# First mixer of a one-core fp32 layer stack: values of four heads opened in 512-wide matmuls, a new order of the later values and of one gate tile, and recurrence steps emitted within a tick

## The chip, the core and the metric

The kernel runs on one core of a Trainium2 chip. The metric is the device time of one execution in microseconds (us); several executions give a median. Five engines matter: TensorE (PE, with its weight loads shown as PEld), VectorE (DVE), ScalarE (ACT), GpSimd (POOL) and SyncE (SP), which issues the loads. TensorE's clock has two levels, 1.2 and 2.4 GHz, and the profile gives the granted share of the upper one (PEclk). Each engine runs its own instructions in the order in which the program emitted them, and waits for the others through semaphores.

## What is computed

The reference is a layer stack on x of 1024 tokens by 1024 features: a gated linear recurrence (the first mixer), an MLP, a dilated attention (the second mixer), a second MLP. The change lies in the first mixer alone, which is, cut to what matters:

```
proj = h @ w_in;  q, f, i, g = split(proj, 4)          # 8 heads of 128
k  = (1 - lb) * sigmoid(-f);  log_f = log(lb + (1 - lb) * sigmoid(f))
qf = silu(q) * 128 ** -0.5
S_t = diag(f_t) S_{t-1} + k_t v_t^T;   o_t = S_t^T q_t    # v = i, per head
o  = o * rsqrt(mean(o^2) + eps) * out_norm * silu(g)
return o @ w_out
```

## The kernel before, in words

All products are fp32 made of three fp32r matmuls (`mm3`, L212 to L214: high by high, high by low and low by high parts). The tile is 128 rows of contraction by 128 by 512 or 256 columns. Weights come as slabs of 128 by 1024 through `use` and `split_next`: a load (SP), a cast of the high part (ACT, L175) and a subtraction for the low part (DVE, L178).

The recurrence of a head is made parallel: within 32 tokens directly (`diag`), then by levels that join blocks (`level0`, `level1`, `level2`, then `level(16)`, `level(32)`, `level(64)`), and over chunks of 128 tokens by states (`krt` transposes the keys, `states`, `outs`), with a norm and a turn (`scale`, `final`) at the end. Each level issues a small group of matmuls that scores queries `qf` against keys `kr` (L367 and L413 and L485), and then on DVE brings both forward: `advance` (L401 to L403) and `queries` (L386 to L390) for the queries, `keys` (L442, L443), `totals` (L432 to L434) for the decays, `keep` (L420) which copies scores under a mask, and L492 to L494 for the three upper levels. So each level reads on PE what DVE wrote in the level before.

These steps are emitted between the large matmuls. `unit` (24 matmuls of 512 columns) and `unit_b` (48 of 256 columns in two halves) call `tick` in their middle or at the end of each half; `tick` runs what stands in the plan for that slot, in the order in which it was put there. The table `SCAN_AT` gives each of the twelve steps of a head its tick, counted from the end of the head's queries. A head takes 8 ticks (four units: f in two halves, q in two halves), and the steps of a head stretch over 24, so steps of two or three heads interleave. Two heads share one pair of value tiles: before heads 0, 2, 4 and 6 the values of the pair are computed 256 columns wide with tokens on rows (192 matmuls), then f and q of both heads. I call these stretches pair 1 (heads 0 and 1) to pair 4; the values that follow a pair (or the gate tiles after pair 4) run while its second head's steps are due. For f, DVE scales the bank (L609), ACT makes `f`, `kr` and `f` again (L783 to L785). For q, DVE scales (L609), ACT takes a sigmoid (L794), and DVE multiplies (L795) into `qf`.

The program opens with the values of heads 0 and 1 for the first 512 tokens, one slice of contraction at a time as x and the weights arrive.

Of the kernel before, what the change touches and what calls it, by code (L numbers as in the profile page):

```python
# [11 lines left out]
F32 = mybir.dt.float32  # L12
F32R = mybir.dt.float32r
# [7 lines left out]
P = 128  # L21
# [76 lines left out]
class Kernel:  # L98
    def __init__(self, tc, ctx, x, w, consts, masks, tab, out):
        self.tc, self.nc = tc, tc.nc  # L100
        self.low = self.nc.vector
        self.x_dram, self.w_dram, self.c_dram = x, w, consts
        self.m_dram, self.tab_dram, self.out_dram = masks, tab, out
        cp = ctx.enter_context(tc.tile_pool(name="consts", bufs=1))
        self.cp = cp
        self.sm = ctx.enter_context(tc.tile_pool(name="small", bufs=2))
        self.tp = ctx.enter_context(tc.tile_pool(name="tmp", bufs=N_TMP))
        self.slots = Slots(ctx.enter_context(tc.tile_pool(name="slots", bufs=1)), N_SLOTS)
        self.acc = ctx.enter_context(tc.tile_pool(name="acc", bufs=4, space=bass.MemoryType.PSUM))
# [36 lines left out]

    def tick(self):
        while self.slot in self.plan:
            for fn in self.plan.pop(self.slot):
                fn()  # L150
        self.slot += 1

    def drain(self):
        while self.plan:
            self.tick()
# [198 lines left out]
    def hgrn_scan(self, h, qf, kr, f, v):  # L354
# [15 lines left out]
        def diag():  # L370
            ps = small(self.bank(), lambda t: qf[:, t:t + 32], 32)
            ve.copy_predicated(ac, self.masks[:, M_DIAG:M_N], ps)
            st["tots"] = S.get("tots")

# [17 lines left out]
        def advance(i, half, tot):  # L392
            b = B4[i]
            n = HALF // (4 * b)
            r = st.pop((i, half))
            rv = r[:, :768].rearrange("p (v n b) -> p v n b", v=6, b=b)
# [6 lines left out]
            ve.tensor_tensor(qv[:, 2:4], rv[:, 3::2], d0, op=MUL)  # L403
            S.put(r)

# [63 lines left out]
        def level(b):  # L469
# [4 lines left out]
            if b == 16:  # L474
                pv = small(ps, lambda t: qv[:, t // (2 * b):(t + 32) // (2 * b), 1, :], 16)
                ve.copy_predicated(ac.rearrange("p (n two b) -> p n two b", two=2, b=b)[:, :, 1, :],
                                   self.masks[:, M_16:M_DIAG].rearrange("p (n b) -> p n b", b=b),
                                   pv.rearrange("p (n b) -> p n b", b=b))
            else:
# [43 lines left out]

        t = SCAN_AT
        for i, fn in enumerate((diag, level0, level1, level2)):
            self.at(t[i], fn)
        for i in range(3):
            self.at(t[4 + i], lambda i=i: level(16 << i))
        for i, fn in enumerate((krt, states, outs, scale, final)):
            self.at(t[7 + i], fn)  # L530

# [110 lines left out]
    def run(self):  # L642
# [3 lines left out]
        x = [S.get("x") for _ in range(KT)]  # L646
        wst = [S.get("w") for _ in range(2)]
        self.next_load = 2

# [3 lines left out]

        def load_w(i, c0=0, n=HALF):
            c = slice((i % 2) * HALF + c0, (i % 2) * HALF + c0 + n)
            nc.sync.dma_start(wst[i // 2][:, c], self.w_dram[i // 2][:, c])

# [3 lines left out]
        load_w(0, 256, 256)  # L661
        load_x(1, 0)
        load_w(1)
        load_x(2, 0)
        load_x(3, 0)
        load_w(2)
        load_x(4, 0)
        load_x(5, 0)
        load_w(3)
        load_x(6, 0)  # L670
        load_x(7, 0)
        for k in range(KT):
# [25 lines left out]
        zs = [None, None]  # L698
        vs = [S.get("v"), S.get("v")]
        ws = [(S.get("hi", F32R), S.get("lo", F32R)) for _ in range(2)]  # L700
        banks = [self.accb() for _ in range(4)]

        def split_w(k, n):
            hi, lo = ws[k // 4]
            c = slice((k % 4) * 256, (k % 4) * 256 + n)
            nc.scalar.copy(hi[:, c], wst[k // 4][:, c])
            nc.vector.tensor_tensor(lo[:, c], wst[k // 4][:, c], hi[:, c].bitcast(F32), op=SUB)

        for k in range(KT):
            if k == 0:  # L710
                split_w(0, 256)
            self.split_x(x[k], self.col(C_NMIX + k), u[k], 0)
            if k and (k == 1 or k % 2 == 0):
                split_w(k, 256 if k == 1 else 512)
# [7 lines left out]
        S.put(*wst)  # L722
        self.next_split = self.next_use = 2
        self.at(0, self.split_next)
        for k in range(KT):
# [3 lines left out]
        bp = [self.bank() for _ in range(2)]  # L729
        self.unit_b(ws, u, 2, bp[0])  # L730
        self.col_b(ws, u, 6, range(KT), bp[1][:, :256])
        zs[0] = self.norm_rows(sqs, 0, self.rb, delay=0)
        for k in range(KT):
            self.square_in(x[k], k, 1, sqs, engine=nc.vector)
        for t in range(4):
            self.values1(banks[t], t, vs, zs[0])
        self.col_b(ws, u, 7, range(KT), bp[1][:, 256:])
        self.tick()
        self.blocks = sm.tile([P, P], F32R, name="blocks")
        self.ones = sm.tile([P, P], F32R, name="ones")  # L740
# [20 lines left out]
        def second_half():  # L761
            zs[1] = self.norm_rows(sqs, 1, self.rb, delay=1)
            for p in range(2):
                self.values(bp[p], 2 + p, vs, zs)
            S.put(*x, sqs)

        self.at(2, second_half)
        self.done(ws)
        for h in range(8):
            if h % 2 == 0 and h:  # L770
                vs = [S.get("v"), S.get("v")]
                ws = self.use(2)
                for p in range(4):
                    ps = self.unit_b(ws, u, p)
                    self.values(ps, p, vs, zs)
                self.done(ws)
            f, kr, qf = S.get("f"), S.get("kr"), S.get("qf")
# [11 lines left out]
            for half in range(2):  # L789
# [11 lines left out]
        for j in range(8):  # L801
# [7 lines left out]
            self.done(ws)  # L809
        self.drain()  # L810
        S.put(*self.a_bufs, self.rb)
# [957 lines left out]
```

## Time and profile before

| | us |
|---|---|
| median of 3 runs (lowest to highest) | 2263.52 (2262.01 to 2264.18) |
| the profiled execution, its own time | 2263.14 |
| its span in the profile | 2261.4 |
| PE busy | 2233.7 (99%) |
| DVE busy | 1775.9 (79%) |
| ACT busy | 856.0 (38%) |

The first mixer fills about the first 450 us of the span. PE is the engine that is nearly always busy, so time is read from PE: what its large matmuls take from one start to the next, and every stretch in which it stands. A PE row with idle time before it names in brackets what released it. The ends of matmuls are modelled and overlap, so the path is read from start to start.

### The profile page before, as it was taken

Reading aid. Unit: us, or ns where it says so; the run is one execution under the profiler, and the core shown is the slowest. Engines: PE = TensorE matmul, PEld = TensorE weight load, DVE = VectorE, ACT = ScalarE, POOL = GpSimd, SP = SyncE. Lnnn points to the kernel's source line nnn. Section 1 sums busy time; section 2 is a strip of 40 time slices with the busy share of each in tenths; the row PEclk is TensorE's granted clock in tenths of the full one; section 3 lists DMA queues with packets and bytes.
Section 4 is the critical chain, followed back from the end, with each engine's and each line's share of the span. In section 5 each row is a group of like instructions: output and inputs, shape, how many; then the busy total and the mean of one; then the engine's idle time right before and its main releaser. Section 6 shows DMA issues by size and latency. Waiting matters only on the chain.

```text
span 2261.4 us, 32861 instructions
## 1 busy us (share of the span) xinstructions
PE 2233.7 (99%) x13102; PEld 1883.5 (83%) x13102; DVE 1775.9 (79%) x2674; ACT 856.0 (38%) x1259; POOL 347.0 (15%) x340
## 2 busy tenths in 40 slices
PE   8999999999999999999999999999999999999998
PEld 7888897888888888888889888888888888888887
DVE  6757668736988888989996556885798888889896
ACT  6333333434433335433344232224533333634322
POOL 0020101101111111222210011000111111222223
PEclk9999999999999999999999999999999999999999
DMA  5001011122344448544514101113334445744442
GB/s 182 30 29 39 20 39 39 47 85 112 128 175 157 153 167 291 167 140 160 194 38 187 38 29 46 39 38 118 125 135 177 149 151 212 263 142 155 153 158 75
DMA packets 82521, 270.30 MB, mean 120 GB/s; under 512 B 9152, under 2 KB 11712, under 8 KB 82368
## 3 DMA queue, kind: packets, MB, share of 16 engines
q1 hardware_dynamic: 81792, 267.67, 33.8%
q8 instruction: 103, 1.69, 0.3%
q10 hardware_dynamic: 576, 0.52, 0.1%
q14 instruction: 50, 0.41, 0.1%
HBM read 190.57 MB, written 77.59 MB: 119 GB/s over the span
## 4 chain that ended last, share of the span: by engine, by line
PE 89%; DVE 8%; ACT 2%; issue 1%; DMA 0%; SPq 0%; DVEq 0%; ACTq 0%
PE acc L212 21%; PE acc L213 21%; PE acc L214 21%; PE ps L212 7%; PE ps L213 7%; PE ps L214 7%; PE ps L574 1%; PE ps L576 1%; PE ps L554 1%; DVE ac L420 1%; DVE lo L178 1%; DVE tmp L609 1%; DVE r L389 0%; PE ps L485 0%; PE ps L539 0%
## 5 line engine op out<-in xcount | busy, mean ns | idle before, releaser
L212 PE MATMUL acc<-hi,hi 128*128 128x512 f32 (+1 forms) x824 | 315.1, 382 | 0.5 <-ACT acc L1255 0.4
L214 PE MATMUL acc<-hi,lo 128*128 128x512 f32 (+1 forms) x824 | 313.8, 381 | 0.0
L213 PE MATMUL acc<-lo,hi 128*128 128x512 f32 (+1 forms) x824 | 313.8, 381 | 0.0
L212 PE MATMUL acc<-uh,hi 128*128 128x512 f32 x768 | 305.6, 398 | 0.0
L214 PE MATMUL acc<-uh,lo 128*128 128x512 f32 x768 | 299.4, 390 | 0.0
L213 PE MATMUL acc<-ul,hi 128*128 128x512 f32 x768 | 299.1, 389 | 0.0
L212 PE MATMUL ps<-hi,hi 128*128 128x512 f32 x712 | 277.2, 389 | 0.0
L214 PE MATMUL ps<-hi,lo 128*128 128x512 f32 x712 | 277.0, 389 | 0.0
L213 PE MATMUL ps<-lo,hi 128*128 128x512 f32 x712 | 277.0, 389 | 0.0
L1198 ACT ACTIVATE hq<-hq 128x512 f32<-128x512 f32 x128 | 81.0, 634 | 333.3 <-DVE hq L1197 267.3
L212 PEld LDWEIGHTS acc<-hi,hi 128*128 128x128 f32 x824 | 154.9, 188 | 31.4 <-ACT acc L1255 1.1
L214 PEld LDWEIGHTS acc<-hi,lo 128*128 128x128 f32 x824 | 154.9, 188 | 29.8
L213 PEld LDWEIGHTS acc<-lo,hi 128*128 128x128 f32 x824 | 154.9, 188 | 29.7 <-issue 0.2
L214 PEld LDWEIGHTS acc<-uh,lo 128*128 128x128 f32 x768 | 144.1, 188 | 30.8
L212 PEld LDWEIGHTS acc<-uh,hi 128*128 128x128 f32 x768 | 144.2, 188 | 30.0 <-ACT v L638 0.2
L213 PEld LDWEIGHTS acc<-ul,hi 128*128 128x128 f32 x768 | 144.3, 188 | 28.7 <-issue 0.5
L214 PEld LDWEIGHTS ps<-hi,lo 128*128 128x128 f32 x712 | 133.6, 188 | 28.0
L212 PEld LDWEIGHTS ps<-hi,hi 128*128 128x128 f32 x712 | 133.6, 188 | 27.7
L213 PEld LDWEIGHTS ps<-lo,hi 128*128 128x128 f32 x712 | 133.7, 188 | 27.6
L189 ACT CAST hi<-h 128x1024 fp32r<-128x1024 f32 x96 | 100.4, 1055 | 134.0 <-DVE lo L190 76.5
L190 DVE TENSOR_TENSOR lo<-h,hi 128x1024 fp32r<-128x1024 f32 x96 | 122.1, 1280 | 6.3 <-ACT hi L189 6.3
L178 DVE TENSOR_TENSOR lo<-w,hi 128x1024 fp32r<-128x1024 f32 x74 | 89.8, 1219 | 28.4 <-ACT hi L175 28.3
(278 smaller groups left out, 4644.3 us busy)
## 6 DMA issues: line engine op xcount, KB each, us to landing
w<-in_w SPq DMA_DIRECT2D x202, 512.0 KB, 4.5
hf<-f SPq DMA_DIRECT2D x28, 512.0 KB, 2.6
hfull<-hq SPq DMA_DIRECT2D x28, 512.0 KB, 3.5
hg<-g SPq DMA_DIRECT2D x28, 512.0 KB, 4.1
h<-hfull SPq DMA_DIRECT2D x28, 512.0 KB, 3.6
h<-hf SPq DMA_DIRECT2D x28, 512.0 KB, 4.4
h<-hg SPq DMA_DIRECT2D x28, 512.0 KB, 3.4
xs<-x SPq DMA_DIRECT2D x16, 512.0 KB, 2.8
```

Source lines behind the costliest of these rows:

```text
L178: self.low.tensor_tensor(lo, st, hi.bitcast(F32), op=SUB)
L189: self.nc.scalar.copy(hi, src)
L190: self.low.tensor_tensor(lo, src, hi.bitcast(F32), op=SUB)
L212: mm(ps, lhsT=ah, rhs=bh, start=start, stop=False)
L213: mm(ps, lhsT=ah, rhs=bl, start=False, stop=False)
L214: mm(ps, lhsT=al, rhs=bh, start=False, stop=stop)
L420: ve.copy_predicated(av[:, j:], mask[:, v0:v1], pm[:, v0:v1])
L554: nc.tensor.matmul(ps[:, c * P:(c + 1) * P], lhsT=kt[:, t], rhs=v[:, t], start=True, stop=True)
L574: nc.tensor.matmul(o, lhsT=a3[:, i, :], rhs=v[:, t], start=True, stop=(i == 0))
L576: nc.tensor.matmul(o, lhsT=qx[:, t], rhs=s[:, t], start=False, stop=True)
L609: self.nc.vector.tensor_tensor(z, ps, self.rb[:, half * HALF:(half + 1) * HALF], op=MUL)
L1198: nc.scalar.activation(t, t, AF.Square)
```

## The change

1. The opening computes the values of heads 0 to 3, 512 columns wide, with four weight slabs loaded in alternation with x. Tokens 768 to 1023 of it run as two plain units of 24 matmuls (t = 6 and 7).
2. A table, `HGRN_ORDER`, gives the order: heads 0, 1, values 4 and 5, heads 2, 3, values 6 and 7, heads 4, 5, gate tile 0, heads 6, 7, gate tiles 1 to 7. The weights in DRAM are laid out accordingly.
3. `defer` puts a step behind a number of units of `mm3` work within a tick (one unit is one 512-wide triple, or two 256-wide ones); `mm3` counts and `tick` empties the list. `SCAN_LATE` gives each step its deferral: `diag` 2, `level0` 1, `level(32)` 1, `level(64)` 1, `outs` 1. Inside `level2` the scores, the keys and the mask copy come 2 units after the advance; in `level(16)` what follows the matmuls comes 1 unit after them.
4. The product of the first half of q moves to the next tick. Tiles `r` are freed later and `tots` is taken in `level0`.

```diff
+HGRN_ORDER = (("h", 0), ("h", 1), ("v", 4), ("h", 2), ("h", 3), ("v", 6), ("h", 4), ("h", 5), ("g", 0),
+              ("h", 6), ("h", 7), *(("g", j) for j in range(1, 8)))
+
+SCAN_LATE = (2, 1, 0, 0, 0, 1, 1, 0, 0, 1, 0, 0)
...
     def tick(self):
+        self.flush()
         while self.slot in self.plan:
...
+    def defer(self, n, fn):
+
+        self.late.append((self.work + n, fn))
+        self.late.sort(key=lambda e: e[0])
+
+    def flush(self, upto=float("inf")):
+        while self.late and self.late[0][0] <= upto:
+            self.late.pop(0)[1]()
...
         mm(ps, lhsT=al, rhs=bh, start=False, stop=stop)
+        self.work += bh.shape[-1] / HALF
+        self.flush(self.work)
...
         def level2():
-            keep = scores(1)
             for half in range(2):
                 advance(1, half, st["d1"])
-            keys(1, st["d1"], st["e1"])
-            keep()
+
+            def rest():
+                keep = scores(1)
+                for half in range(2):
+                    S.put(st.pop((1, half)))
+                keys(1, st["d1"], st["e1"])
+                keep()
+
+            self.defer(2, rest)
...
+        steps = (diag, level0, level1, level2, *(lambda i=i: level(16 << i) for i in range(3)),
+                 krt, states, outs, scale, final)
+        for i, (fn, n) in enumerate(zip(steps, SCAN_LATE)):
+            self.at(t[i], (lambda fn=fn, n=n: self.defer(n, fn)) if n else fn)
...
         load_w(0, 0, 256)
         nc.sync.dma_start(self.cs, self.c_dram)
         load_x(0, 0)
         load_w(0, 256, 256)
...
+        for k in range(1, KT):
+            load_w(k)
+            load_x(k, 0)
...
+        def values_k(t, k, ps):
+            hi, lo = ws[k // 2]
+            c = slice((k % 2) * HALF, (k % 2 + 1) * HALF)
+            tk = slice(t * P, (t + 1) * P)
+            uh, ul = u[k]
+            self.mm3(ps, uh[:, tk], ul[:, tk], hi[:, c], lo[:, c], k == 0, k == KT - 1)
...
             for t in range(4):
-                self.col_b(ws, u, t, (k,), banks[t][:, :256])
+                values_k(t, k, banks[t])
...
-                nc.vector.scalar_tensor_tensor(qf[:, tk], z, self.c1[:, h:h + 1], sg, op0=MUL, op1=MUL)
-                if half == 1:
-                    self.hgrn_scan(h, qf, kr, f, vs[h % 2])
+
+                def product(tk=tk, z=z, sg=sg):
+                    nc.vector.scalar_tensor_tensor(qf[:, tk], z, self.c1[:, h:h + 1], sg, op0=MUL, op1=MUL)
+
+                if half == 0:
+                    self.at(0, product)
+                else:
+                    self.flush()
+                    product()
+                    self.hgrn_scan(h, qf, kr, f, vs[h])
```

What this does to the order on the engines is shown at three places of pair 2. The first is DVE where `level(64)` of head 2 meets `level1` of head 3 (`kr_1454` before and `kr_1484` after are the keys of head 2; `qf_1704`, `kr_1703` and `qf_1742`, `kr_1741` are queries and keys of head 3). Before:

```order
L434 TENSOR_TENSOR tots_2178<-f_1702,tmp_2187 128x256 [waits DVE_49]
L178 TENSOR_TENSOR lo_2216<-w_1705,hi_2215 128x1024 [waits DMAHW3_49,Activation_49]
L492 TENSOR_TENSOR tots_1808<-tots_1808 128x8
L493 TENSOR_TENSOR kr_1454<-kr_1454,tots_1808 128x8x64 [waits PE_49]
L494 TENSOR_TENSOR qf_1455<-qf_1455,tots_1808 128x8x64
L401 TENSOR_TENSOR qf_1704<-qf_1704,f_1702 128x128
...
L442 TENSOR_TENSOR kr_1703<-kr_1703,tmp_2187 128x256x2 [waits PE_49]
...
L434 TENSOR_TENSOR tots_2178<-tots_2178,tmp_2313 128x64 [waits DVE_49]
```

The same place after:

```order
L451 TENSOR_TENSOR tots_2188<-f_1740,tmp_2197 128x256 [waits DVE_49]
L391 COPY_PREDICATED ac<-masks,ps_2207 128x256 [waits PE_49]
L195 TENSOR_TENSOR lo_2254<-w_1743,hi_2253 128x1024 [waits DMAHW7_49,Activation_49]
L419 TENSOR_TENSOR qf_1742<-qf_1742,f_1740 128x128
...
L459 TENSOR_TENSOR kr_1741<-kr_1741,tmp_2197 128x256x2 [waits PE_49]
...
L451 TENSOR_TENSOR tots_2188<-tots_2188,tmp_2338 128x64 [waits DVE_49]
L522 TENSOR_TENSOR tots_1815<-tots_1815 128x8
L523 TENSOR_TENSOR kr_1484<-kr_1484,tots_1815 128x8x64 [waits PE_49]
L524 TENSOR_TENSOR qf_1485<-qf_1485,tots_1815 128x8x64
```

The keys of head 2's `level(64)` (L493 before, L523 after) moved from ahead of head 3's `level1` to behind it.

The second place is DVE where `level2` of head 2 ends (`keys`, then `keep`) and the low part of a weight slab and a scaled bank of the next unit stand. Before:

```order
L403 TENSOR_TENSOR qf_1455<-r_1898,tots_1808 128x2x32x4
L442 TENSOR_TENSOR kr_1454<-kr_1454,tmp_1907 128x64x8 [waits PE_49]
L443 TENSOR_TENSOR kr_1454<-kr_1454,tots_1808 128x64x4
L420 COPY_PREDICATED ac<-masks,ps_1958 128x3x16x4
...
L178 TENSOR_TENSOR lo_2001<-w_1604,hi_2000 128x1024 [waits DMAHW2_49,Activation_49]
L609 TENSOR_TENSOR tmp_2004<-acc_1930,rb_146 128x512
```

The same place after:

```order
L421 TENSOR_TENSOR qf_1485<-r_1936,tots_1815 128x2x32x4
L195 TENSOR_TENSOR lo_2001<-w_1642,hi_2000 128x1024 [waits DMAHW6_49,Activation_49]
L637 TENSOR_TENSOR tmp_2004<-acc_1968,rb_152 128x512 [waits PE_49]
L459 TENSOR_TENSOR kr_1484<-kr_1484,tmp_1945 128x64x8 [waits PE_49]
L460 TENSOR_TENSOR kr_1484<-kr_1484,tots_1815 128x64x4
L437 COPY_PREDICATED ac<-masks,ps_2015 128x3x16x4
```

The keys of `level2` moved from ahead of the low part `lo_2001` and the scaled bank `tmp_2004` to behind both.

The third place is PE in the first half of the values that follow pair 2, from `final` of head 1 (L603, L631) over `level(32)` of head 2 (L485, L511) to `diag` of head 3 (L367, L386) and `krt` of head 2 (L539, L567); between the rows stand 256-wide matmuls. Before:

```order
L603 MATMUL ps_2116<-cs,os_1955 128x128 x4
L485 MATMUL ps_2122<-qf_1455,kr_1454 32x32 x16
L367 MATMUL ps_2144<-qf_1704,kr_1703 32x32 x32
...
L485 MATMUL ps_2248<-qf_1455,kr_1454 64x64 x8
L413 MATMUL ps_2261<-r_2179,kr_1703 32x6x8 x16
...
L539 MATMUL ps_2371<-cs,kr_1454 128x128 x4
```

The same place after:

```order
L631 MATMUL ps_2154<-cs,os_1993 128x128 x4
...
L511 MATMUL ps_2166<-qf_1485,kr_1484 32x32 x16
...
L386 MATMUL ps_2207<-qf_1742,kr_1741 32x32 x32
...
L430 MATMUL ps_2286<-r_2189,kr_1741 32x6x8 x16
...
L511 MATMUL ps_2348<-qf_1485,kr_1484 64x64 x8
...
L567 MATMUL ps_2409<-cs,kr_1484 128x128 x4
```

What stood together now stands apart, with 6 of the 256-wide matmuls ahead of and behind `level(32)`, and 90 of them between L511 of `level(32)` and L567, where before 96 stood between L485 of `level(32)` and L539. Over the whole program PE has 10119 rows before and 9927 after, 192 fewer; the small groups break into the large matmuls of the first mixer 58 times before and 75 times after.

## Rows read from the trace of the kernel before

**Rows 1.** The view by stretches of the span: the stretch in us, its length, busy us and (instructions) of PE, PEld, DVE, ACT, POOL, then PEclk, the DMA share and GB/s. The stretches are the ones that hold the stalls of pairs 1 to 4 and of the gate tiles behind pair 4.

```profile
80.00:95.00 15.00, 13.39 (x236) 12.00 (x235) 13.42 (x29) 8.02 (x16) 0.00 (x0) 1.00 0.24 72
...
150.00:200.00 50.00, 47.39 (x681) 42.10 (x680) 40.60 (x85) 18.73 (x37) 6.33 (x12) 0.97 0.11 34
...
250.00:300.00 50.00, 47.39 (x748) 42.11 (x748) 43.97 (x94) 18.61 (x39) 6.33 (x12) 1.00 0.11 34
...
345.00:400.00 55.00, 52.27 (x681) 42.59 (x681) 48.17 (x102) 18.94 (x32) 6.35 (x12) 1.00 0.09 31
400.00:450.00 50.00, 48.74 (x341) 41.51 (x329) 33.92 (x65) 19.44 (x34) 10.31 (x24) 1.00 0.14 43
```

**Rows 2.** The view of waits, 0 to 450 us: who waited for what, us in total, times, the longest.

```profile
PE ps L485 <- DVE qf L494: 4.1, 5, 1.0
PE ps L367 <- DVE qf L795: 4.0, 4, 1.0
```

**Rows 3.** The timeline of PE in the opening: start, duration, engine, line, operation, tiles, and in brackets the idle time before and its releaser.

```profile
5.51 0.58 PE L212 MATMUL acc<-hi,uh 128*128 128x256 f32 x1 [5.51 <-ACT uh L287]
...
9.71 0.58 PE L213 MATMUL acc<-lo,uh 128*128 128x256 f32 x1 [0.24 <-DVE lo L707]
...
14.99 0.28 PE L213 MATMUL acc<-lo,uh 128*128 128x256 f32 x1
```

**Rows 4.** The timeline of ACT in the opening: the cast of the second slice of x, which waited for its load, and a cast of 256 columns of weights.

```profile
7.82 0.72 ACT L287 ACTIVATE uh<-x,cs 128x512 fp32r<-128x512 f32 x1 [2.35 <-DMA x<-in_x]
8.44 0.39 ACT L706 CAST hi<-w 128x256 fp32r<-128x256 f32 x1
```

**Rows 5.** The timeline of PE: two neighbours 512 columns wide, two 256 wide, from two undisturbed stretches.

```profile
164.20 0.39 PE L214 MATMUL acc<-uh,lo 128*128 128x512 f32 x1
164.43 0.39 PE L212 MATMUL acc<-uh,hi 128*128 128x512 f32 x1
...
178.41 0.28 PE L212 MATMUL acc<-hi,uh 128*128 128x256 f32 x1
178.53 0.28 PE L213 MATMUL acc<-lo,uh 128*128 128x256 f32 x1
```

**Rows 6.** The timeline of PE through pair 2: the small groups and the large matmuls next to them.

```profile
169.64 0.39 PE L214 MATMUL acc<-uh,lo 128*128 128x512 f32 x1
170.64 0.76 PE L413 MATMUL ps<-r,kr 128*32 128x48 f32 x53 [0.61 <-DVE kr L443]
...
176.82 0.39 PE L214 MATMUL acc<-uh,lo 128*128 128x512 f32 x1
177.29 0.72 PE L367 MATMUL ps<-qf,kr 128*32 128x16 f32 x64
...
182.86 0.64 PE L485 MATMUL ps<-qf,kr 128*32 128x32 f32 x29 [0.90 <-DVE qf L494]
...
184.82 0.46 PE L367 MATMUL ps<-qf,kr 128*32 128x32 f32 x32 [1.01 <-DVE qf L795]
...
185.69 0.42 PE L212 MATMUL acc<-hi,uh 128*128 128x256 f32 x1
...
189.08 0.28 PE L213 MATMUL acc<-lo,uh 128*128 128x256 f32 x1
...
192.43 0.28 PE L214 MATMUL acc<-hi,ul 128*128 128x256 f32 x1
192.64 1.15 PE L485 MATMUL ps<-qf,kr 128*64 128x64 f32 x16
...
200.39 0.93 PE L539 MATMUL ps<-cs,kr 128*128 128x128 f32 x7
```

**Rows 7.** The timeline of DVE through pair 2: where `level0` of head 2 begins and ends, then `keys` of `level2`, the low part and the scaled bank behind it, then the steps of `level(32)` (L492 at 184.68), `level(64)` (L493) and `level1` of head 3 from 195.03 to 204.00.

```profile
156.50 0.83 DVE L386 TENSOR_TENSOR r<-qf,f 128x384 f32<-128x384 f32 x1
...
162.01 1.21 DVE L178 TENSOR_TENSOR lo<-w,hi 128x1024 fp32r<-128x1024 f32 x1
163.15 0.68 DVE L609 TENSOR_TENSOR tmp<-acc,rb 128x512 f32<-128x512 f32 x1
...
176.13 0.69 DVE L442 TENSOR_TENSOR kr<-kr,tmp 128x512 f32<-128x512 f32 x1
...
177.06 0.97 DVE L420 COPY_PREDICATED ac<-masks,ps 128x192 f32<-128x192 uint8 x3
...
184.68 0.17 DVE L492 TENSOR_TENSOR tots<-tots 128x16 f32<-128x16 f32 x1
...
185.97 0.44 DVE L372 COPY_PREDICATED ac<-masks,ps 128x256 f32<-128x256 uint8 x1
186.31 0.86 DVE L386 TENSOR_TENSOR r<-qf,f 128x384 f32<-128x384 f32 x1
...
193.82 0.69 DVE L493 TENSOR_TENSOR kr<-kr,tots 128x512 f32<-128x512 f32 x1 [0.64 <-PE ps L485]
...
195.03 0.38 DVE L401 TENSOR_TENSOR qf<-qf,f 128x128 f32<-128x128 f32 x1
...
204.00 0.28 DVE L402 TENSOR_TENSOR qf<-r,tots 128x128 f32<-128x128 f32 x1
```

**Rows 8.** The timeline of ACT in pair 2: the first activation for `f` and the cast of the high part of the next slab, which stands behind the three activations.

```profile
173.98 0.64 ACT L783 ACTIVATE f<-tmp 128x512 f32<-128x512 f32 x1 [5.39 <-DVE tmp L609]
...
175.75 1.04 ACT L175 CAST hi<-w 128x1024 fp32r<-128x1024 f32 x1
```

More of the change, by code (lines that the diff above doesn't have):

```diff
@@ L112, in __init__ @@
         self.plan = defaultdict(list)
+        self.late = []
+        self.work = 0.0
         self.n = 0
@@ L151, in tick @@
         self.slot += 1
+    def defer(self, n, fn):
[4 more added lines that the diff above has]
+            self.late.pop(0)[1]()
     def drain(self):
-        while self.plan:
+        while self.plan or self.late:
             self.tick()
@@ L372, in diag @@
             ve.copy_predicated(ac, self.masks[:, M_DIAG:M_N], ps)
-            st["tots"] = S.get("tots")
         def queries(i, half, tot):
@@ L394, in advance @@
             n = HALF // (4 * b)
-            r = st.pop((i, half))
+            r = st[i, half]
             rv = r[:, :768].rearrange("p (v n b) -> p v n b", v=6, b=b)
@@ L447, in level0 @@
         def level0():
+            st["tots"] = S.get("tots")
             for half in range(2):
@@ L455, in level1 @@
                 advance(0, half, f)
+                S.put(st.pop((0, half)))
                 queries(1, half, st["d1"])
@@ L524, in hgrn_scan @@
         t = SCAN_AT
[L525 to L530, printed above, removed]
+        steps = (diag, level0, level1, level2, *(lambda i=i: level(16 << i) for i in range(3)),
+                 krt, states, outs, scale, final)
+        for i, (fn, n) in enumerate(zip(steps, SCAN_LATE)):
+            self.at(t[i], (lambda fn=fn, n=n: self.defer(n, fn)) if n else fn)
     def transpose7(self, src, dst, scale):
@@ L646, in run @@
         x = [S.get("x") for _ in range(KT)]
-        wst = [S.get("w") for _ in range(2)]
-        self.next_load = 2
+        wst = [S.get("w") for _ in range(4)]
+        self.next_load = 4
         def load_x(k, half):
@@ L652, in load_x, with load_w @@
             nc.sync.dma_start(x[k][:, tk], self.x_dram[k, :, tk])
-        def load_w(i, c0=0, n=HALF):
-            c = slice((i % 2) * HALF + c0, (i % 2) * HALF + c0 + n)
-            nc.sync.dma_start(wst[i // 2][:, c], self.w_dram[i // 2][:, c])
+        def load_w(k, c0=0, n=HALF):
+            c = slice((k % 2) * HALF + c0, (k % 2) * HALF + c0 + n)
+            nc.sync.dma_start(wst[k // 2][:, c], self.w_dram[k // 2][:, c])
         load_w(0, 0, 256)
@@ L698, in run, with split_w, values_out @@
         zs = [None, None]
-        vs = [S.get("v"), S.get("v")]
-        ws = [(S.get("hi", F32R), S.get("lo", F32R)) for _ in range(2)]
+        vs = [S.get("v") for _ in range(4)]
+        ws = [(S.get("hi", F32R), S.get("lo", F32R)) for _ in range(4)]
         banks = [self.accb() for _ in range(4)]
[L703 to L707, printed above, removed]
+        def split_w(k, c0=0, n=HALF):
+            hi, lo = ws[k // 2]
+            c = slice((k % 2) * HALF + c0, (k % 2) * HALF + c0 + n)
+            nc.scalar.copy(hi[:, c], wst[k // 2][:, c])
+            nc.vector.tensor_tensor(lo[:, c], wst[k // 2][:, c], hi[:, c].bitcast(F32), op=SUB)
+        def values_k(t, k, ps):
+            hi, lo = ws[k // 2]
+            c = slice((k % 2) * HALF, (k % 2 + 1) * HALF)
+            tk = slice(t * P, (t + 1) * P)
+            uh, ul = u[k]
+            self.mm3(ps, uh[:, tk], ul[:, tk], hi[:, c], lo[:, c], k == 0, k == KT - 1)
+        def values_out(t, ps):
+            for i in range(4):
+                nc.scalar.activation(vs[i][:, t * P:(t + 1) * P], ps[:, i * P:(i + 1) * P], AF.Copy,
+                                     scale=zs[t // 4][:, t % 4:t % 4 + 1])
         for k in range(KT):
             if k == 0:
-                split_w(0, 256)
+                split_w(0, 0, 256)
             self.split_x(x[k], self.col(C_NMIX + k), u[k], 0)
-            if k and (k == 1 or k % 2 == 0):
-                split_w(k, 256 if k == 1 else 512)
+            if k == 0:
+                split_w(0, 256, 256)
+            else:
+                split_w(k)
             for t in range(4):
-                self.col_b(ws, u, t, (k,), banks[t][:, :256])
+                values_k(t, k, banks[t])
         nc.vector.reciprocal(d, e)
@@ L729, in run @@
         bp = [self.bank() for _ in range(2)]
-        self.unit_b(ws, u, 2, bp[0])
-        self.col_b(ws, u, 6, range(KT), bp[1][:, :256])
+        for k in range(KT):
+            values_k(4, k, bp[0])
         zs[0] = self.norm_rows(sqs, 0, self.rb, delay=0)
@@ L735, in run @@
         for t in range(4):
-            self.values1(banks[t], t, vs, zs[0])
-        self.col_b(ws, u, 7, range(KT), bp[1][:, 256:])
+            values_out(t, banks[t])
+        for k in range(KT):
+            values_k(5, k, bp[1])
         self.tick()
+        self.at(0, self.split_next)
         self.blocks = sm.tile([P, P], F32R, name="blocks")
@@ L763, in second_half, with values_pair, head @@
             for p in range(2):
-                self.values(bp[p], 2 + p, vs, zs)
+                values_out(4 + p, bp[p])
             S.put(*x, sqs)
-        self.at(2, second_half)
-        self.done(ws)
[L769 to L776, printed above, removed]
+        self.at(0, second_half)
+        for t in (6, 7):
+            ps = self.accb()
+            for k in range(KT):
+                values_k(t, k, ps)
+                if k == 3:
+                    self.tick()
+            self.tick()
+            values_out(t, ps)
+        self.done(ws)
+        def values_pair():
+            ws = self.use(2)
+            v = [S.get("v"), S.get("v")]
+            for p in range(4):
+                ps = self.unit_b(ws, u, p)
+                self.values(ps, p, v, zs)
+            self.done(ws)
+            return v
+        def head(h):
             f, kr, qf = S.get("f"), S.get("kr"), S.get("qf")
@@ L794, in run, with gate_tile @@
                 nc.scalar.activation(sg, z, AF.Sigmoid)
-                nc.vector.scalar_tensor_tensor(qf[:, tk], z, self.c1[:, h:h + 1], sg, op0=MUL, op1=MUL)
-                if half == 1:
-                    self.hgrn_scan(h, qf, kr, f, vs[h % 2])
+                def product(tk=tk, z=z, sg=sg):
+                    nc.vector.scalar_tensor_tensor(qf[:, tk], z, self.c1[:, h:h + 1], sg, op0=MUL, op1=MUL)
+                if half == 0:
+                    self.at(0, product)
+                else:
+                    self.flush()
+                    product()
+                    self.hgrn_scan(h, qf, kr, f, vs[h])
             self.done(ws)
         y = []
-        for j in range(8):
+        def gate_tile(j):
             ws = self.use()
@@ L809, in run @@
             self.done(ws)
+        for step, i in HGRN_ORDER:
+            if step == "v":
+                vs += values_pair()
+            else:
+                (head if step == "h" else gate_tile)(i)
         self.drain()
@@ L1720 @@
     sv = slabs2(wi[:, 2048:3072])
-    w = []
-    for p in range(4):
-        w += [sv[2 * p], sv[2 * p + 1], sf[2 * p], sq[2 * p], sf[2 * p + 1], sq[2 * p + 1]]
+    w = list(wi[:, 2048:2560].reshape(4, 2, P, 512).transpose(0, 2, 1, 3).reshape(4, P, 1024))
+    for step, i in HGRN_ORDER:
+        w += {"v": list(sv[i:i + 2]), "h": [sf[i], sq[i]], "g": [sg[i]]}[step]
     pairs = [0, 4, 1, 5, 2, 6, 3, 7]
-    w += list(sg) + [slabs(a["hgrn_w_out"][0])[j] for j in pairs]
+    w += [slabs(a["hgrn_w_out"][0])[j] for j in pairs]
     def mlp(w1, w2):
```

24 lines of the change are left out of this document (8 added, 16 removed).

## The prediction

> **What bounds the kernel now.** PE is busy 99% of the span, so a microsecond counts only where PE's large matmuls come later or take longer. I read first the stretches of the span: outside the opening, PE stands only where a pair's second head meets its steps, and in the gate tiles behind pair 4. In the five stretches of [rows 1] PE lacks 1.61, 2.61, 2.61, 2.73 and 1.26 us, 10.8 in all. Then the waits [rows 2]: the names are those of the recurrence, scores that wait for queries which DVE has just multiplied (L485 on L494, L367 on L795). Then the timeline of PE in pair 2 [rows 6]: L413 starts 1.00 after the matmul ahead of it where 0.21 is normal (192.43 to 192.64), so that stall costs 0.8; the next ones cost 0.25 (177.29), 1.06 (182.86) and 1.20 (184.82), 3.28 from start to start against 2.61 of idle time. The same ratio, 1.25, on 10.8 gives **13.5 us of stalls on the path**. Last the clock: only the stretch with pair 2 has a granted clock of 0.97 [rows 1]; there the 16 large matmuls from 185.69 to 189.08 take 0.21 each, at the 1.2 GHz level, where 0.12 is normal [rows 5, 6], 1.5 us. The stalls of pairs 3 and 4 are as long and no dip follows them.
>
> Since DVE is 79% busy over the span and 40 to 48 of 50 to 55 us in these stretches [rows 1], and does its rows in the order of the program, what decides is which DVE row stands ahead of the one that PE waits for.
>
> **The change part by part.** The sum is made against the profiled execution, 2263.14 us, 0.4 below the median of the runs shown.
>
> *Opening, and wide values.* 384 matmuls of 256 columns become 192 of 512. At full clock two cost 0.24 and one 0.227 [rows 5]: 192 x 0.013 = **2.5 us** saved. The Trainium skill (TensorE: Matmul & The Clock Gate, section Back-to-back issue gap) puts the gap at a fixed 2.5 ns above the columns' time, by which a merge would save only 2.7 ns, an estimate of 0.5 us in all; the rows here show more, and the sum goes by them. Before, PE starts at 5.51, waits twice (the second slice of x was cast only at 7.82), restarts at 9.71 and is at full clock from 14.99, 5.3 later [rows 3, 4]. After, the first product needs a second cast of 256 columns (0.39, [rows 4]), so it starts near 5.9; but a slice of contraction is then 12 matmuls of 0.43 at the lower level, 5.1 us of work, and the second slice is due only near 11, about 3 us after its x landed before; one more load of weights ahead of it (some 0.7) is hidden. So no gap follows, and 5.3 us after a start that is steady from about 6.7 the clock is up near 12.0, 3 us earlier. In those 3 us PE works at twice the speed, and it lost 1.3 in gaps before, less the later start: I take **1.6 us** saved (0.9 to 2.4).
>
> *The old stalls.* The pieces that waited now stand apart from what they wait for, by 6 to 18 large matmuls: all 13.5 go, and the dip behind two of them (1.5) with them. What is late next is DVE, below.
>
> *Interruptions.* The small groups break into the stream 75 times instead of 58. A step into a group takes 0.21 instead of 0.12 (192.43 to 192.64, [rows 6]), and the step out about as much more: 17 x 0.16 = **2.7 us** (1.5 to 5).
>
> *krt behind the next head's level1.* L567 transposes keys that L523 of `level(64)` has multiplied. Before, that row stood ahead of the next head's `level1` (193.82 against 195.03, [rows 7]) and was done six microseconds before PE came for it at 200.39 [rows 6]. Now it stands behind it. From the end of PE's `level(32)` group DVE must do: its three rows 1.3 (184.68 to 185.97), `level0` 5.5 (156.50 to 162.01), the mask copy 0.35, the low part 1.15, `level1` 9.0 (195.03 to 204.00), then two rows 0.7: **18.0 us**. PE meanwhile has 90 matmuls of 0.12 = 10.8, the groups of `diag`, `level1` and `level(64)` (0.46, 0.76, 1.15 by [rows 6]) and three steps in and out of 0.3: **14.1 us**. It waits 3.9 in pairs 1 and 2. In pair 3 the gate tile that replaces the values adds a DVE product (0.7, as L609 in [rows 7]) and a sigmoid table on ACT, behind which the copies for `queries` stand; no row shows that place, I take 1.1 (0 to 1.5): 5.7. In pair 4 the scaled products of the head before fall in too: 6.4. Together 19.9 (bounds: 2.7 each, were the ACT copies inside `level1`, 0.6 twice, to come for nothing, 10.8; or 6.4 each, 25.6).
>
> *level(16) behind the low part.* L386 needs `keys` of `level2`. Before, these came at 176.13, ahead of the low part [rows 7]; now the low part comes first, and it needs the cast that stands on ACT behind the three activations and ends at 176.79 [rows 8]. With `outs` deferred one unit, and `diag`'s copy behind `level0`, that chain runs up to 0.8 later: 177.6, then 1.15 for the low part, 0.6 for the scaled bank, 0.9 for `keys` (176.13 to 177.06): 180.3. PE, without its stall of 0.8 but with 0.4 for the split groups, comes at 176.7. It waits **3.6** (2.8 without the 0.8) in pairs 2 and 3; in pair 1 the cast comes earlier and in pair 4 PE comes later, where I take 0.9 and 0.5 (0 to 3.6 each): 8.6 (5.6 to 14.4).
>
> *Pair 4's outputs* now follow `scale` and `keep` on DVE: 2.0 (0 to 2.0). The product of q's first half moves to the next tick: DVE does it in the same gap, nothing, or 0.7 (its duration) where DVE is late, which is inside the bounds above.
>
> *Clock.* Six of the new stalls last 3.6 us or more, three times the old ones. After one of three old places the clock fell for 1.5 us of loss. I take four dips, **6.0 us** (0 to 9). The Trainium skill (TensorE: Matmul & The Clock Gate, section Part 1: The HAM clock gate) says that an idle array goes back to 1.2 GHz and that activity frees it again. By that rule each of the six would dip; the trace agrees at 185.69 and not behind the stalls of pairs 3 and 4, which were short.
>
> *Sum.* -2.5 - 1.6 - 13.5 - 1.5 + 2.7 + 19.9 + 8.6 + 2.0 + 6.0 = **+20.1, 2283 us**.
>
> **The rivals.**
> 1. *It does what it says.* Each read on PE stands far enough behind its write: the old 15.0 go, nothing comes: -2.5 - 1.6 - 15.0 + 2.7 = -16.4, **2247 us**. The point that decides is whether DVE's 18.0 us between `level(32)` and the keys of `level(64)` fit under PE's 14.1: DVE would have to be 3.9 us quicker there. For it: PE's old waits are all on rows that do get further away. Against: DVE's rows from 184.68 to 204.00 follow one another nearly without a gap [rows 7].
> 2. *New stalls at their lower bounds*, no dips: krt 10.8, `level(16)` 5.6: -16.4 + 16.4 = 0, **2263 us**.
> 3. *The stalls come, the clock stays up*: +14.1, **2277 us**. For it: two of three old places show no dip.
> 4. *Every long stall drops the clock*: six times 1.5: **2286 us**, and with the other terms at their upper bounds up to some 2297.
>
> **How the numbers follow.** Chances: forecast 0.42, rival 1 0.16, rival 2 0.12, rival 3 0.15, rival 4 0.15. A difference under 0.2% (4.5 us) can't be told from none: faster is rival 1, 0.16; same is rival 2, 0.12; slower is the rest, 0.72. The range leaves out rival 1 and the top of rival 4: 2260 to 2293.
>
> **What would show it.** In the waits of the changed kernel: L567 on L523 four times, about 4 us each and more in pairs 3 and 4; L386 on L460 twice with 3 to 4 us; no wait of L511 on L524 or L386 on L844 worth a microsecond. In the stretches: PE lacks some 7 us in each of pairs 2 to 4 where it lacked 2.6, and the granted clock falls below 1.00 there. In the opening: no gap after 6.7 and full clock near 12. I am wrong if L567 starts right behind the matmul ahead of it in pairs 1 and 2: then DVE reaches `level(64)` earlier than its order says, and rival 1 or 2 holds.

## The result, and the profile after

| | us |
|---|---|
| before, median of 4 runs | 2262.77 (2261.92 to 2264.18) |
| after, median of 4 runs | 2292.27 (2290.61 to 2293.12) |
| ratio after to before | 1.0134, 95% interval 1.0122 to 1.0147 |
| profiled execution after, its own time and its span | 2290.61, 2288.8 |

The change makes the kernel 30 us slower (28 to 33 by the interval). The forecast was 20 slower, 2283, with a range up to 2293; the ratio on the median shown before gives 2293.9, just above that range. The profiled execution is the lowest of its four, so the rows below explain 27.5 us (2290.61 against 2263.14).

The view by stretches of the kernel after (columns as in [rows 1]); `krt` of the first head of pairs 1 to 4 now starts at 127, 231, 335 and 426 us:

```profile
95.00:150.00 55.00, 50.23 (x758) 46.12 (x757) 36.48 (x83) 17.99 (x43) 0.00 (x0) 0.97 0.10 31
150.00:210.00 60.00, 56.15 (x530) 47.37 (x529) 40.52 (x82) 21.10 (x34) 11.75 (x24) 0.94 0.08 27
210.00:260.00 50.00, 46.02 (x625) 42.50 (x624) 30.70 (x67) 18.04 (x40) 5.41 (x12) 0.97 0.13 44
260.00:310.00 50.00, 46.15 (x470) 38.35 (x469) 33.47 (x69) 15.22 (x26) 6.33 (x12) 0.98 0.07 22
310.00:360.00 50.00, 43.72 (x516) 35.85 (x515) 35.05 (x75) 21.03 (x37) 1.74 (x3) 0.91 0.10 33
360.00:420.00 60.00, 57.28 (x692) 46.15 (x690) 46.35 (x95) 18.84 (x32) 7.07 (x22) 1.00 0.09 28
420.00:470.00 50.00, 44.00 (x375) 37.15 (x376) 33.82 (x67) 18.31 (x32) 4.69 (x12) 0.93 0.09 33
```

PE lacks 31.5 us in these stretches, about three times what it lacked in [rows 1], and the granted clock is below 1.00 in six of the seven, where it was in one. The view of waits (80 to 480 us) has none of the names of [rows 2] left:

```profile
PE ps L567 <- DVE kr L523: 20.8, 4, 6.5
PE ps L386 <- DVE kr L460: 8.5, 3, 3.9
PE ps L631 <- DVE tmp L449: 1.6, 1, 1.6
```

The timeline of PE through pair 2, against [rows 6]:

```profile
200.03 0.39 PE L231 MATMUL acc<-uh,lo 128*128 128x512 f32 x1
204.27 0.94 PE L386 MATMUL ps<-qf,kr 128*32 128x16 f32 x54 [3.85 <-DVE kr L460]
...
205.64 0.42 PE L230 MATMUL acc<-lo,uh 128*128 128x256 f32 x1
...
209.45 0.28 PE L230 MATMUL acc<-lo,uh 128*128 128x256 f32 x1
...
226.27 0.28 PE L231 MATMUL acc<-hi,ul 128*128 128x256 f32 x1
230.53 1.73 PE L567 MATMUL ps<-cs,kr 128*128 128x128 f32 x7 [3.98 <-DVE kr L523]
```

`level(16)` (L386) starts 4.24 after the matmul ahead of it, then 17 large matmuls run at the 1.2 GHz level (205.64 to 209.27, 0.21 each); `krt` (L567) starts 4.26 after, and its group takes 1.38 to the next large matmul (231.91), where 0.68 was taken before (200.39 to 201.07): it runs at the lower clock too. DVE beside it, against [rows 7]:

```profile
200.35 0.42 DVE L421 TENSOR_TENSOR qf<-r,tots 128x256 f32<-128x256 f32 x1
201.37 1.23 DVE L195 TENSOR_TENSOR lo<-w,hi 128x1024 fp32r<-128x1024 f32 x1 [0.59 <-ACT hi L192]
202.51 0.68 DVE L637 TENSOR_TENSOR tmp<-acc,rb 128x512 f32<-128x512 f32 x1
203.11 0.68 DVE L459 TENSOR_TENSOR kr<-kr,tmp 128x512 f32<-128x512 f32 x1
203.71 0.42 DVE L460 TENSOR_TENSOR kr<-kr,tots 128x256 f32<-128x256 f32 x1
...
229.44 0.26 DVE L451 TENSOR_TENSOR tots<-tots,tmp 128x64 f32<-128x64 f32 x1
229.62 0.16 DVE L522 TENSOR_TENSOR tots<-tots 128x8 f32<-128x8 f32 x1
229.70 0.68 DVE L523 TENSOR_TENSOR kr<-kr,tots 128x512 f32<-128x512 f32 x1
```

DVE stands at the low part until ACT's cast is there, and only then makes the keys that PE waits for; and the keys of `level(64)` come right behind the last row of the next head's `level1`. From start to start the new waits are 0.95, 4.14 (pair 1), 4.01, 4.14 (pair 2), 4.01, 6.44 (pair 3), 1.77, 0.76, 6.68 (pair 4): 32.9 us.

The opening, against [rows 3]:

```profile
5.87 0.80 PE L229 MATMUL acc<-hi,uh 128*128 128x512 f32 x1 [5.87 <-ACT hi L727]
...
7.29 0.63 PE L231 MATMUL acc<-hi,ul 128*128 128x512 f32 x1
7.72 0.63 PE L229 MATMUL acc<-hi,uh 128*128 128x512 f32 x1
...
11.51 0.40 PE L229 MATMUL acc<-hi,uh 128*128 128x512 f32 x1
```

It starts 0.36 later, has no gap behind 7.29, and is at full clock from 11.5 in place of 15.

### The profile page after: what moved, and what is told of

Same layout as the page of the kernel before. It is cut to its first block, busy times and chain, and to the rows that moved or that the text cites. A ratio compares the mean times of both kernels' runs of the same rounds, so it can differ in the third digit from the quotient of the medians.

```text
span 2288.8 us, 32477 instructions
## 1 busy us (share of the span) xinstructions
PE 2240.7 (98%) x12910; PEld 1878.3 (82%) x12910; DVE 1775.2 (78%) x2676; ACT 858.1 (37%) x1263; POOL 343.1 (15%) x340
## 4 chain that ended last, share of the span: by engine, by line
PE 89%; DVE 8%; ACT 2%; issue 1%; DMA 0%; SPq 0%; DVEq 0%; ACTq 0%
PE acc L229 21%; PE acc L230 20%; PE acc L231 20%; PE ps L229 7%; PE ps L231 7%; PE ps L230 7%; PE ps L602 1%; PE ps L604 1%; PE ps L582 1%; DVE ac L437 1%; DVE r L407 1%; DVE lo L195 1%; PE ps L567 1%; PE ps L511 0%; DVE r L404 0%
```

## The experiments

Each run is compared with the kernel before on its own chip. Edits are told against the changed kernel.

| run | median, us | ratio to before (95%) | PE's waits, us | clock dips, large matmuls, us | small groups at 1.2 GHz, us |
|---|---|---|---|---|---|
| kernel before | 2262.77 | | 13.5 | 1.4 | 0.0 |
| changed kernel | 2292.27 | 1.0134 (1.0122 to 1.0147) | 32.9 | 7.0 | 2.9 |
| `level(64)` first | 2273.27 | 1.0049 (1.0034 to 1.0064) | 19.7 | 4.0 | 3.2 |
| keys first | 2284.58 | 1.0098 (1.0083 to 1.0113) | 29.1 | 5.2 | 1.8 |
| both first | 2261.78 | 0.9999 (0.9990 to 1.0009) | 13.7 | 1.0 | 0.2 |
| no deferral | 2269.06 | 1.0033 (1.0020 to 1.0046) | 19.1 | 3.0 | 2.5 |
| both, final later | 2260.12 | 0.9993 (0.9983 to 1.0002) | 12.4 | 1.6 | 0.0 |
| both, gate earlier | 2264.39 | 1.0013 (1.0003 to 1.0022) | 15.8 | 1.6 | 0.0 |
| two apart | 2265.45 | 1.0015 (1.0006 to 1.0025) | 16.3 | 0.0 | 4.5 |
| low parts on GpSimd | 2265.11 | 1.0016 (1.0006 to 1.0025) | 15.3 | 1.0 | 3.1 |
| both, turns earlier | 2256.21 | 0.9978 (0.9969 to 0.9987) | 10.2 | 0.0 | 0.0 |
| no deferral, turns earlier | 2259.22 | 0.9993 (0.9984 to 1.0002) | 12.3 | 0.0 | 1.4 |
| turns earlier, outs at tick | 2256.61 | 0.9979 (0.9970 to 0.9988) | 8.4 | 0.0 | 0.0 |
| three apart | 2255.42 | 0.9975 (0.9966 to 0.9984) | 7.7 | 0.0 | 1.7 |

The last three columns are worked out from the timeline of PE, 60 to 480 us, of the profiled execution: what steps beside a small group take above the normal step, where that is 0.24 us or more; what runs of large matmuls at the 1.2 GHz level lose; and what the steps inside small groups lose where the granted clock is 0.50, against the same steps at full clock. The medians of the kernel before lay between 2260.84 and 2262.67 in the three sets of runs. In the expectations of the last two runs, the first and the second run are "both, turns earlier" and "no deferral, turns earlier".

**`level(64)` first.** `-SCAN_LATE = (2, 1, 0, 0, 0, 1, 1, 0, 0, 1, 0, 0)`, `+SCAN_LATE = (2, 1, 0, 0, 0, 1, 0, 0, 0, 1, 0, 0)`

> Theory A (place of the write on VectorE): only the deferral of level(64) is taken back, so its keys stand ahead of the next head's level1 again. The four waits of the krt transposes (4.1, 4.1, 6.4 and 6.7 us in the changed kernel) go, and the clock dips behind them (0.9, 0.5, 1.0, 1.4 us): 2292.3 - 21.4 - 3.8 = about 2267 us. The two level(16) waits of 4.0 stay. Theory B (VectorE is simply full in these stretches, so a wait that is taken away comes back at the next read): 5 us or less come back, 2287 us or more. Theory C (the new order of values and gate tile, with its table loads, costs the time): no change in pairs 1 and 2, 2285 us or more.

The waits of 4.14 in pairs 1 and 2 are gone without a rest, as theory A said, but the waits fall by only 13 of the 21 us: 2.9 come back in pair 3 at `level(16)`, and in pair 4 `krt` still waits 4.84, now not for its keys.

**Keys first.** `-self.defer(2, rest)`, `+rest()`

> Only the deferral inside level2 is taken back, so its keys stand ahead of the low part of the next weight slab and of the scaled bank again. Theory A: the level(16) waits (0.95, 4.0, 4.0 us) go, with their two clock dips of 1.6: 2292.3 - 9.0 - 3.2 = about 2280 us; the krt waits stay at 4 to 7 us. Theory B: the gain comes back at the scores of level(32) or at diag, 2288 us or more.

The three `level(16)` waits go, 9.0 us; 4.9 return earlier and later in pairs 2 and 3, at the scores of `level2` (1.4 each) and at `level(32)` (0.9 and 1.1). Here theory B holds for a half: the cause of a wait was DVE's order, and DVE was late for the next read as well.

**Both first**, the two edits together.

> Both edits together. Theory A: the waits of krt (21.4) and of level(16) (9.0) go, and all six dips (7.0): 2292.3 - 37.4 = about 2255 us, faster than the kernel before by some 8, since its own waits (13.5) don't return: the groups stay apart. What stays is 2.5 us of waits in pair 4 and the interruptions. Theory B (VectorE is full): 2275 us or more. Theory D (the groups set apart cost more than the waits they avoid): 2263 us or more, with no wait over 1 us left in pairs 1 to 3.

30 us come back, but it is no faster than the kernel before, and theory A's 2255 is missed by 7: waits of 5.6 us stand in pairs 2 and 3, mostly at the scores of `level2` and at `level(32)`, and 7.8 in pair 4. The largest rest is the 4.85 in pair 4. Its timeline, PE and then DVE:

```profile
385.35 0.89 PE L430 MATMUL ps<-r,kr 128*32 128x48 f32 x64 [0.28 <-DVE ac L391]
391.75 1.03 PE L631 MATMUL ps<-cs,os 128*128 128x128 f32 x8
392.62 0.60 PE L567 MATMUL ps<-cs,kr 128*128 128x128 f32 x4
397.90 0.80 PE L567 MATMUL ps<-cs,kr 128*128 128x128 f32 x3 [4.69 <-DVE tmp L449]
```

```profile
395.54 2.22 DVE L437 COPY_PREDICATED ac<-masks,ps 128x192 f32<-128x192 uint8 x3
397.46 0.35 DVE L449 TENSOR_TENSOR tmp<-tots 128x64 f32<-128x64 f32 x1
```

The small groups share four PSUM banks in turn (`ps2`, `bufs=4`). L430 takes one, L631 two, the first half of `krt` the fourth; the second half needs the first again, and starts when DVE's masked copies (L437) have read it; the bracket names the row that DVE began behind them. These groups belong to three heads (7, 5 and 6) and need no data of each other.

**No deferral**: `SCAN_LATE` all zero, and `level2`, `level(16)` and the first half's product emitted at their tick, as before.

> All deferrals are taken back, also that of the first half's product; the wide opening and the new order of values and gate tile stay. Theory A: the waits of the kernel before return (13.5 us and a dip of 1.5), the new ones (32.9 and 7.0 of dips) and the 17 interruptions go; what is left is the saving of the opening and of the wide values, 2.3 + 2.3: about 2258 us (2256 to 2261). Theory C (order and table loads cost): 2275 us or more.

The waits of the kernel before are back in pairs 1 to 3, yet it is 7 us slower than before: in pair 4 `final` waits 3.8 and `krt` 4.8, and 5.5 us go to the clock, 2.5 of them in small groups. So the new order costs by itself. The gate tile in the third gap is 4 ticks long where the values were 8, and brings `final` of heads 4 and 5 against the scores and `krt` of heads 6 and 7.

**Both, final later**: both first, and

```
-self.at(t[i], (lambda fn=fn, n=n: ...
+self.at(t[i] + 2 * (h == 5 and i == 11), (lambda fn=fn, n=n: ...
```

> As the run with both deferrals taken back (2261.8 us), and the turn of head 5 (final, two PSUM banks) moves two ticks later, behind the krt of head 6. Theory E (PSUM ring): in pair 4 the gate tile, a gap of 4 ticks in place of 8, brings final of head 5 into the same tick as krt of head 6, so that the second transposes of krt reuse the bank of head 7's first scores and wait 4.85 us for DVE's masked copy of them. Then that wait goes, and its clock dip of 1.0: about 2256 us. Rival F (krt there waits for ACT, which stands in the gate tile's activations, or for the DVE write of the keys): the wait stays where it is, 2261 us or more.

`krt` waits no more, so the bank was the cause, but `final` now stands last in the same ring and waits 2.4 for ACT, which copies `krt`:

```profile
PE ps L631 <- ACT krt L570: 2.3, 1, 2.3
```

**Both, gate earlier**: both first, and `("g", 0)` and `("v", 6)` change places in `HGRN_ORDER`.

> As the run with both deferrals taken back, and the gate tile moves from the third gap to the second, the values 6 and 7 from the second to the third. Theory E: the short gap decides; the 4.85 us wait of krt in pair 4 (behind head 6) goes, and the same wait appears behind the second gap, in pair 3, unless the head of two pairs before has its final elsewhere: the total stays within 3 us of 2262. Rival G (pair 4 waits because gate tiles follow it): the 4.85 us stay in pair 4, and the other pairs are as they were.

The wait moves with the short gap, from pair 4 to pair 3, as theory E said; gate tiles behind a pair don't make it:

```profile
299.37 0.60 PE L567 MATMUL ps<-cs,kr 128*128 128x128 f32 x4
303.82 0.52 PE L567 MATMUL ps<-cs,kr 128*128 128x128 f32 x3 [3.84 <-DVE tmp L449]
```

**Two apart**: no deferral but `SCAN_LATE = (2, 0, 0, 0, 0, 1, 0, 0, 0, 0, 0, 0)`, and final of head 5 later.

> No deferrals but two: diag by 2 units and level(32) by 1, and final of head 5 two ticks later. Against the run without deferrals (2269.1 us): the waits of L511 on level(16)'s queries (0.7 to 1.1 per pair) and of diag on the product (1.2 per pair) go, 8.5 us, but for some 0.3 each; eight groups more break into the stream at 0.4 each, 3.2 us; the krt wait of 4.8 in pair 4 goes, with 1 us of dip: about 2258 us. Theory B (VectorE is full, the waits come back at the next read): 2264 us or more.

A miss. The waits at `diag` go and those at `level(32)` fall to 0.4 to 0.8, but `level(64)` now waits 2.2 and 2.3 in pairs 2 and 3 on L525, `level(32)`'s rows on DVE, which stand behind `level0` when they alone are deferred. And 4.5 us go to the clock in small groups: it is granted at 0.50 from 210.4 to 213.8 and from 364.0 to 370.8.

**Low parts on GpSimd**: as both, final later, with `self.low = nc.gpsimd` around the loop over `HGRN_ORDER`.

> As the run with final of head 5 later, and the low parts of the weight slabs of the first mixer's heads, values and gate tiles are subtracted on GpSimd in place of VectorE. Theory B (VectorE's queue is what the remaining 8 us of waits stand for): each of pairs 2 to 4 has two low parts of 1.15 us ahead of the reads that wait, so 5 to 7 us go: about 2250 us. Rival H (GpSimd's longer operation holds VectorE up, or the low parts land too late for the large matmuls): no gain or a loss, 2256 us or more.

No gain: rival H. On GpSimd, and then on DVE in the same stretch, and the same DVE row in the run with the low parts on VectorE:

```profile
180.65 2.40 POOL L195 TENSOR_TENSOR lo<-w,hi 128x1024 fp32r<-128x1024 f32 x1
```

```profile
180.68 2.63 DVE L419 TENSOR_TENSOR qf<-qf,f 128x128 f32<-128x128 f32 x1
```

```profile
181.74 0.39 DVE L419 TENSOR_TENSOR qf<-qf,f 128x128 f32<-128x128 f32 x1
```

DVE's row took 2.63 in place of 0.39 while GpSimd's ran. Here DVE was freed of 1.15 and lost 2.2.

**Both, turns earlier**: both first, and

```
+self.at(t[i] - (h in (4, 5)) * {10: 2, 11: 3}.get(i, 0), (lambda fn=fn, n=n: ...
```

> Both deferrals taken back (2261.8 us), and scale and final of heads 4 and 5 come two and three ticks earlier, so that their two PSUM banks are taken ahead of the first scores of heads 6 and 7. Theory E (PSUM ring): the waits of pair 4 at final (1.75) and at krt (4.85) both go, with the dip of 1.0, and none comes in their place, unlike with final later: about 2254 to 2256 us. Rival: the earlier norm is not ready (its chain on GpSimd is some 5 us), and final waits for it by 1 to 3 us: 2258 us or more.

The two waits and the dip are gone, as theory E said, and this is the only version so far clearly faster than before. But others came in pair 4: `outs` waits 1.6 for its states, and `level(32)` (L511) 1.8 for its queries.

**No deferral, turns earlier**: the same line in the kernel without deferrals.

> No deferrals (2269.1 us), with the same earlier scale and final of heads 4 and 5. What then differs from the kernel before is the wide opening and the new order alone. Theory E: 3.8 and 4.8 us of waits and 3.0 of dips in pairs 3 and 4 go, pair 4 keeps 5 us as before: about 2258 us, 4 to 5 under the kernel before, which is the opening (2.3) and the wide values (2.3). Rival C (the gate tile in the gap costs by itself): 2262 us or more.

9 us under the run without it, by the ratios to the kernel before. What is left of the change, opening and order, is then 1.6 us under the kernel before, where 4 to 5 were expected; the interval includes no difference. Against before, `outs` of pair 4 waits 2.6 for its states, and its groups lose 1.4 at the 1.2 GHz level behind that wait.

**Turns earlier, outs at tick**: `SCAN_LATE = (2, 1, 0, 0, 0, 1, 0, 0, 0, 0, 0, 0)`.

> As the first run of this call, and outs is not deferred. Theory: the deferral of outs makes DVE's reductions, level0 and level1 of the next pair some 0.6 later, so that the first scores of level2 (L430) wait 1.4 in place of 0.8: 0.6 us less in pairs 2 and 3 each, and an interruption of 0 to 0.4 less: 1 to 2 us under that run. Rival: no change, since DVE is behind for another reason.

The scores of `level2` wait 0.8 in place of 1.4 in both pairs, as expected, and the time stays: `outs` of pair 4 waits 2.3 in place of 1.6.

**Three apart**: no deferral, turns earlier, and the `SCAN_LATE` of the run above.

> As the second run of this call with three deferrals: diag 2, level0 1, level(32) 1. With level0 deferred too, level(32)'s keys stay ahead of level0 on DVE, so the waits of 2.2 at level(64) that the run with diag and level(32) alone had don't come; the waits of the kernel before at level(32) and diag (1.9 to 2.3 a pair) fall to 1 or less: 3 to 5 us under the second run of this call, less some 3 us for eight more interruptions: 2256 to 2259 us. Rival B: the waits return elsewhere, 2260 us or more.

The lowest median, 5.6 us under before (3.6 to 7.7 by the interval), with the smallest waits:

```profile
PE ps L605 <- DVE s L589: 2.3, 2, 2.1
PE ps L430 <- DVE kr L460: 1.8, 3, 0.6
PE ps L512 <- DVE qf L525: 0.9, 3, 0.4
PE ps L386 <- DVE kr L460: 0.5, 1, 0.5
```

No run of large matmuls is slow, but behind the wait of 2.3 at `outs` the granted clock is 0.50 from 359.3 to 362.7, and 1.7 us are lost there: two of its 128-wide matmuls step 0.43 until then, and 0.22 afterwards.

```profile
359.97 0.64 PE L603 MATMUL ps<-v,a 128*128 128x128 f32 x2
360.40 0.63 PE L605 MATMUL ps<-s,qf 128*128 128x128 f32 x2
...
363.06 0.39 PE L603 MATMUL ps<-v,a 128*128 128x128 f32 x2
363.28 0.39 PE L605 MATMUL ps<-s,qf 128*128 128x128 f32 x2
```

With `level0` deferred beside it, `level(32)`'s rows stay ahead on DVE, and the 2.2 us of the run with two apart are gone. Its interval overlaps those of the two runs with turns earlier and deferrals, so among the three no order is shown.

## Why the prediction was right or wrong

The direction and both main mechanisms were right; the size was a quarter too small (20.1 forecast, 27.5 between the two profiled executions), and the range ended a little too early. The step that failed is the size of the side effects: the interruptions, at "17 x 0.16 = 2.7", cost 5.3, and of the clock the step "I take four dips" was wrong, since all six long waits were followed by one. Small groups at the lower clock, 2.9 us, and the PSUM banks had no term. With every term at its upper bound the sum is some 2300, where rival 4 says 2297. By its terms:

- **`krt` behind `level1`**: forecast 3.9 in pairs 1 and 2, measured 4.14 and 4.14, and the run with `level(64)` first shows the cause, since both waits vanish. Pairs 3 and 4: 5.7 and 6.4 forecast, 6.44 and 6.68 measured. The 1.1 in pair 3 for a sigmoid table came from no row. The trace after shows the table load, 1.28 on ACT, after which DVE waits 1.31 for the copy, 0.73 more than for the next one (0.58 at 328.71); and the gate tile puts two rows on DVE (L637 and L648, 0.6 each), not one.

```profile
323.88 1.28 ACT L645 ACT_TABLE_LOAD   x1 [7.17 <-DVE tmp L637]
```

```profile
326.24 0.43 DVE L407 TENSOR_TENSOR r<-r,tots 128x256 f32<-128x256 f32 x1 [1.31 <-ACT r L406]
```

  In pair 4 the size was right and its reason only in part: with the order on DVE restored, 4.84 stayed, the PSUM ring, so that the size agreed there in part by luck. The prediction had no term for PSUM banks.
- **`level(16)` behind the low part**: 3.6 forecast, 4.01 and 4.01 measured; 0.9 and 0.95 in pair 1; 0.5 and nothing in pair 4.
- **Outputs of pair 4**: 2.0 forecast, 2.5 measured, but 1.77 of it is L631 waiting for the masked copies, a bank again, not `scale`.
- **The old stalls** went, as forecast, but in "both first", which took the new ones away, 5.6 us of waits stand in pairs 2 and 3 again.
- **Clock**: behind all six long waits the clock fell (0.93, 1.59, 0.45, 1.58, 1.00, 1.40 in large matmuls: 7.0 us against 6.0). Rival 4 was what happened, at 1.2 a dip in place of 1.5; the 2.9 in small groups come on top.
- **Interruptions**: the term that was most mis-sized, "17 x 0.16 = 2.7". Summed over each group and the two steps around it, 46 groups without a wait of the kernel before cost 14.8 us and 61 of the kernel after 20.1, 0.33 each: 5.3 more. The bound given reached 5. The timeline of PE after:

```profile
87.04 0.39 PE L231 MATMUL acc<-uh,lo 128*128 128x512 f32 x1
87.36 0.89 PE L430 MATMUL ps<-r,kr 128*32 128x48 f32 x64
88.17 0.50 PE L229 MATMUL acc<-uh,hi 128*128 128x512 f32 x1
88.51 0.40 PE L230 MATMUL acc<-ul,hi 128*128 128x512 f32 x1
...
169.40 0.39 PE L231 MATMUL acc<-uh,lo 128*128 128x512 f32 x1
169.63 1.72 PE L582 MATMUL ps<-v,krt 128*128 128x128 f32 x14
```

  Into L430 the step is 0.32 where 0.23 is normal, out of it 0.34, and the rest is lost inside the group; into the 128-wide group of L582 it is 0.23, nothing.
- **Opening and wide values**: 1.6 forecast, 1.8 measured (the lost steps of the first 60 us fall from 6.5 to 4.3, less the start 0.36 later); 2.5 forecast, 2.3 by the mean steps of 227.7 and 119.9 ns. The formula that the prediction quotes from the Trainium skill (TensorE: Matmul & The Clock Gate, section Back-to-back issue gap) is given there for isolated matmuls, and a stream that loads weights for each is given about 131 ns at 512 columns; neither is the step of this trace. That both together are worth 4 us is worked out from the trace; a kernel with the opening alone was not run, since four heads' values at the start leave one gap without values.

Sum of the measured terms: -2.3 - 1.8 - 13.5 - 1.4 + 5.3 + 32.9 + 7.0 = +26.2 against 27.5 between the two profiled executions. With the 2.9 of small groups at the lower clock, which these terms leave out, it is 29.1: 1.6 too much stays open.

## What to carry to other kernels

When a step is deferred, read each engine's order, not the one that the step was moved for: a scoring group moved by less than a microsecond of matmuls took its DVE rows behind 9 us of another head's. Replacing a block by one of another length shifts every later step that is timed in ticks, and steps that now fall together may fight over a ring of buffers without sharing data. A group that breaks into a stream has a price (here 0.35 to 0.56 us for groups of 32 and 48 columns), so set groups apart only where they wait for more.

## What the runs showed of the hardware

- In the runs above 16 waits of PE of 3.9 us or more were each followed by a stretch at 1.2 GHz that lost 0.45 to 1.8 us (2.0 in one case). All six waits between 2.4 and 3.8 were followed by a granted clock of 0.50 as well; in three of them it fell on the groups of `outs` near 365 us, where no large matmul ran. Of ten waits between 1.9 and 2.3, two were. The two waits of 1.1 and 1.2 in a row that stood in pair 2 of the kernel before, with its dip, had one in pair 3 of the run without deferrals, and none in that run's pair 2.
- A GpSimd subtraction of 128x1024 (2.40 us) held a VectorE product up for its whole length, 2.63 in place of 0.39. The Trainium skill (SBUF — State Buffer, section Terms) says that the two arbitrate for one port pair and that the loser blocks fully; these rows agree. Not every row is held up: beside the subtraction from 195.38 to 197.93 in the same run, three masked copies and a scaled bank (L437, L637), which read PSUM, took their usual 0.97 and 0.68.
